# Inverse's second product in its own PSUM bank, row exponentials moved, the gate stage in a written order, first rows convolved in two parts, five value buffers

## The chip, the cores and the metric

The kernel runs on one core of a Trainium2 chip. Times are device microseconds of one execution. Five engines work side by side: TensorE (PE, with its weight loads PEld), VectorE (DVE), ScalarE (ACT), GpSimd (POOL) and SyncE (SP), which here only issues transfers. Each works through its own instructions in order.

## The reference, cut to what matters

One step of a two-layer encoder over 2048 prompt tokens and 32 sample tokens, 2080 in all, with 1024 channels. The first layer is a gated delta rule with 8 heads of 128 channels; the second, windowed attention, is not touched by the change.

```python
proj = x @ w_in                                              # q, k, v: 3 x 1024; gate z: 1024; a, b: 2 x 8
qkv, new_buf = causal_conv(proj[..., :CONV_DIM], conv_buf, conv_w)   # 4 taps, then silu
g = -exp(a_log) * softplus(a_in + dt_bias)                   # one decay for each head and token
# the delta rule, in chunks: gcum = cumsum(g)
decay = exp(where(incl, gcum_i - gcum_j, -inf))
lower = where(strict, kbeta k^T * decay, 0); tmat = lower + I
u = triangular_solve(tmat, v * beta);  w = triangular_solve(tmat, kbeta * exp(gcum))
v_new = u - w S;  o = (q exp(gcum)) S + (q k^T * decay) v_new;  S = S exp(glast) + kdec^T v_new
o = o * rsqrt(mean(o * o)) * norm_w * silu(z)
x = layer_norm(alpha * x + o @ w_out)
```

## The kernel before, in words

All of it is one program on one core; `program` (L1644) calls the stages one after the other.

**Projections and convolutions** (`qkv`). The 2080 tokens are five blocks of 416. The 3072 channels of q, k and v are 24 rows of 128. A row of one block is 24 matmuls (8 steps over the input channels, each as three products of float parts, L77, L78, L79, to which both operands were split before) into one PSUM bank. Six banks take turns (`ps`). ACT copies each block (L297) into the row's buffer R; there are two such buffers, so row 2 takes that of row 0. Rows 0 and 1 are multiplied together, block by block, while the activations are still being read and split (L69) and two gate columns are formed (L239, L240). Then each row is convolved: the first tap by ACT (L264), the other three by DVE over all 2083 columns (L266), then tanh on ACT (L269) and a product on DVE (L270), and the row is stored. For q and k, ACT squares it, DVE transposes the squares into R (L279) and sums them (L280); that sum is the last to read R. Weights of later stages are split beside it (L95 on ACT, L96 on DVE, stored by SP at L97).

**Gate stage** (`z`, L299, and `split_gate`, L316). For 8 heads and the blocks 0, 1 and 2 the same 24 matmuls form z; block k of this stage means the k-th of these 24, counted from 0. ACT takes tanh (L309) into zth, DVE multiplies (L310) and combines (L311) into z, and SP stores it (L312). zth and z have two buffers each. The weights of the next head are fetched by SP into w_raw (L46, one buffer), cast by ACT into w_hi (L53), the rest subtracted by POOL into w_lo (L54); w_hi and w_lo have two buffers. SP also stores both for later (L323). Beside it PE gets the first steps of the delta rule for the first two chunks (`Ahead.inverses`, L955): loads of gb and k, decays E (L530 on DVE, L536 on ACT), the product g (L550) and the triangular inverse by 31 elimination steps on DVE (L573, L576). The order of PE is written out, as so many quarter blocks between two steps of `inverses`; that of DVE and ACT is left to the scheduler.

**Delta rule** (`Delta.run`, L795). 17 chunks, one of the 32 sample tokens and 16 of 128. The order on PE, DVE and ACT is written out as a list of generators; `go(v, r, ...)` takes one step of each. At any time three chunks are under way: one gets its outputs, the next one its inverse of blocks, the one after its decays, its product g and its eliminations. Of those POOL does the first 25 columns and DVE the last six (L573, L576, on both engines). `invert` (L646) joins 32 x 32 inverses to 128 x 128 ones through PSUM: y1p (L660), read by ACT (L662), up (L671, L672), read by ACT (L673) and DVE (L675, L676), y2p (L684), read by ACT (L685, L686), u2p and u2q (L693, L694), read by ACT (L695, L696). y1p, up, y2p and u2p use pool pb, which has one bank; u2q uses pool pc, which has two and also serves ks (L703 to L706) and vp (L716, L718). `powers` (L619) takes the exponential of the two gb tiles on ACT (L624); `fade` multiplies k and q by them on DVE (L632). `turn_k` transposes k and scales it on ACT (L589), `turn_v` transposes v on PE (L600). v and z tiles are loaded by SP (L520) into one ring of three buffers, `vz`. Matmuls of the gate's remaining blocks and, later, of the first output projection fill PE between the steps; for the latter SP loads x into r (L1008).

After it come the rest of the output projection, the second layer's projections and the attention, unchanged.

Of the kernel before, what the change touches and what calls it, by code (L numbers as in the profile page):

```python
# [22 lines left out]
NT = NP + NS  # L23
# [134 lines left out]
def drain(gen):  # L158
    for _ in gen:
        pass  # L160


class P1:
# [49 lines left out]
    def qkv(self):  # L213
# [12 lines left out]
        for b in range(NB):  # L226
# [14 lines left out]
            for i in range(2):  # L241
                self.block(Rs[i], self.w0[i], b)
        gates(nc, I, T, G, abT, gtmp, one, self.pt)
        parts = one.tile([128, 8, NT // 32], F32, tag="parts", name="parts")
        early, due = presplit(nc, one, I, T), 0.0
        for i in range(24):
            kind, h = i // 8, i % 8
            if i < 2:
                R = Rs[i]
            else:  # L250
                w = split_weights(nc, self.wp, I["w_in"][i], nc.gpsimd)
                R = self.row(i)
                for b in range(NB):
                    self.block(R, w, b)
            due += 224 / 20 if i >= 4 else 0
# [6 lines left out]
            W = NT + 3  # L262
            y = big.tile([128, NT + 3], F32, tag="y", name="y")
            nc.scalar.activation(y[:], R[:, 0:W], AF.Copy, scale=self.convw[:, i, 0:1])  # L264
            for j in range(1, 4):
                nc.vector.scalar_tensor_tensor(out=y[:], in0=R[:, j:j + W], scalar=self.convw[:, i, j:j + 1], in1=y[:],  # L266
                                               op0=ALU.mult, op1=ALU.add)
# [16 lines left out]
        nc.sync.dma_start(self.O["conv"][:, :, :], self.convo[:])  # L284

# [179 lines left out]
class Delta:  # L465
# [42 lines left out]
    def load(self, ch, name, halves=(0, 1)):  # L508
        nc, T, n = self.nc, self.T, ch.n
        ts = slice(ch.t0, ch.t0 + n)  # L510
        pool, tag, bufs = (self.sml, "vz", 3) if name in "vz" else (self.four, name, 5 if name == "q" else 4)
# [134 lines left out]
    def invert(self, ch):  # L646
# [7 lines left out]
        def new(pool):  # L654
            return pool.tile([128, 8, 64], F32, tag="tr", name="bps")
# [24 lines left out]
        y2p = new(self.pb)  # L680
# [114 lines left out]
    def run(self, chunks, S, first, second, side, done):  # L795
# [46 lines left out]
        for i in range(len(chunks) + 1):  # L842
# [29 lines left out]
            go(a, t, a, t, seen, sq)  # L872
            fill(2 * more)
# [25 lines left out]
            p = gen(self.powers, n2)  # L899
            go(v, r, r, r, g, r, r, v, r, k, r, d)  # L900
            side()
            go(v, w, r, d, p)
# [40 lines left out]
class Ahead(Delta):  # L943
# [11 lines left out]
    def inverses(self, chunks):  # L955
        for ch in chunks:
            tmp = Chunk(ch.t0, ch.n)
            for name in ("gb", "k"):
                self.load(tmp, name)
            yield  # L960
            drain(self.decays(tmp))
            yield
            low = self.lower(tmp)
            next(low)
            yield
            drain(low)
            drain(self.chain(tmp, self.nc.vector, 0, 31))
# [676 lines left out]
def program(tc, I, O, T, G):  # L1644
# [7 lines left out]
    zs = p1.z((0, 1, 2), zp, ("zth", "z"), p1.ps, p1.split_gate(nc.gpsimd))  # L1652
    ahead = Ahead(tc, mid, left, I, O, T, G).inverses(chunks[:2])
    with tc.manual_schedule(engines={mybir.EngineType.PE}):
        for n in (18, 18, 6, 6, 12, 12):
            next(ahead)
            drain(itertools.islice(zs, n))
        drain(ahead)
        drain(zs)
# [52 lines left out]
    ET = mybir.EngineType  # L1712
# [191 lines left out]
```

## Time and profile before

| | |
|---|---|
| three runs | 2224.55, 2231.66, 2234.78 us; median 2231.66 |
| profiled execution | 2230.72 us |
| its span in the profile | 2228.9 us |
| mean granted TensorE clock | 0.983 |
| busy: PE, PEld | 2111.1, 1919.0 us |
| busy: DVE, ACT, POOL | 1479.8, 909.8, 718.5 us |
| L266, 72 convolution steps on DVE | 173.3 us |
| L573, L576 on POOL, 375 steps each | 127.8, 143.0 us |

Busy time counts an engine as working while one of its instructions runs; matmuls overlap, so a busy PE may still be slow. A row of a timeline gives start, duration, engine, line, operation, outputs <- inputs, size, and in brackets how long the engine was idle before it and whose result ended the idle time. Groups ("x4") are runs of like instructions. A "q" behind an engine's name is its instruction queue, where transfers are issued. The granted clock is a share of full speed.

### The profile page before, as it was taken

The numbers are of one execution on the slowest core, as the hardware profiler recorded it, in microseconds if no ns is written. First come the engines' busy times: TensorE is split into PE (matmuls) and PEld (weight loads), VectorE is DVE, ScalarE is ACT, GpSimd is POOL, SyncE is SP. The second block draws the span as 40 slices with busy tenths as digits, with TensorE's granted clock in tenths as the row PEclk, the third lists the DMA queues.
The fourth block names the chain that finished last, engine by engine and source line by source line (L and its number), as shares of the span: only waits on it lengthen the run. The fifth ranks groups of instructions, "written<-read, shape, count | busy, mean of one in ns | idle before, by whom it ended". The sixth has DMA issues, their size and how long they took to land.

```text
span 2228.9 us, 37186 instructions
## 1 busy us (share of the span) xinstructions
PE 2111.1 (95%) x13370; PEld 1919.0 (86%) x13370; DVE 1479.8 (66%) x2765; ACT 909.8 (41%) x2403; POOL 718.5 (32%) x1176
## 2 busy tenths in 40 slices
PE   8999999999989999888789999899999998999997
PEld 6899999999989888887777887899999976888775
DVE  4798877876656688778865665554844566556662
ACT  5555545444422566666651211311311035444441
POOL 1223211161110377777751210000000035566663
PEclk9999999999999999999999999999999999999999
DMA  7656656567865534434746765888788895333321
GB/s 285 211 192 190 206 172 194 183 194 232 260 215 175 170 130 148 150 128 157 238 130 233 247 209 157 290 285 283 254 290 287 270 298 157 103 88 95 91 76 43
DMA packets 348377, 430.00 MB, mean 193 GB/s; under 512 B 78352, under 2 KB 276080, under 8 KB 348176
## 3 DMA queue, kind: packets, MB, share of 16 engines
q1 hardware_dynamic: 311280, 310.22, 43.9%
q10 hardware_dynamic: 36912, 117.40, 15.8%
q8 instruction: 106, 1.74, 0.3%
q14 instruction: 79, 0.65, 0.1%
HBM read 269.45 MB, written 158.44 MB: 192 GB/s over the span
## 4 chain that ended last, share of the span: by engine, by line
PE 71%; DVE 13%; DMA 6%; ACT 5%; issue 3%; SPq 2%; POOL 1%; ACTq 0%; DVEq 0%; POOLq 0%
PE ps L77 8%; PE ps L79 8%; PE ps L78 8%; PE ps L1257 5%; PE ps L1258 5%; PE ps L1259 5%; PE ot L1611 3%; PE po L1498 3%; PE po L1499 3%; PE po L1500 3%; PE S L1590 2%; PE po L1030 2%; PE po L1032 2%; PE po L1031 2%; PE tr L1605 2%
## 5 line engine op out<-in xcount | busy, mean ns | idle before, releaser
L77 PE MATMUL ps<-act_hi,w_hi 128*128 128x416 f32 x1280 | 459.4, 359 | 10.0 <-DVE z L310 5.8
L79 PE MATMUL ps<-act_hi,w_lo 128*128 128x416 f32 x1280 | 450.4, 353 | 2.1 <-POOL w_lo L54 1.2
L78 PE MATMUL ps<-act_lo,w_hi 128*128 128x416 f32 x1280 | 451.7, 353 | 0.0
L77 PEld LDWEIGHTS ps<-act_hi,w_hi 128*128 128x128 f32 x1280 | 242.3, 189 | 14.5 <-DVE z L310 6.1
L79 PEld LDWEIGHTS ps<-act_hi,w_lo 128*128 128x128 f32 x1280 | 242.3, 189 | 6.3 <-POOL w_lo L54 1.7
L78 PEld LDWEIGHTS ps<-act_lo,w_hi 128*128 128x128 f32 x1280 | 243.0, 190 | 2.7
L1257 PE MATMUL ps<-xs_h,w 128*128 128x416 f32 x560 | 199.6, 356 | 11.4 <-DVE ra L1314 7.4
L1258 PE MATMUL ps<-xs_l,w 128*128 128x416 f32 x560 | 199.9, 357 | 3.2 <-DVE xs_l L1160 3.2
L1259 PE MATMUL ps<-xs_h,w 128*128 128x416 f32 x560 | 198.5, 355 | 0.0
L54 POOL TENSOR_TENSOR w_lo<-w_raw,w_hi 128x1024 fp32r<-128x1024 f32 x32 | 83.9, 2622 | 343.0 <-ACT w_hi L53 342.9
L266 DVE SCALAR_TENSOR_TENSOR y<-R,convw,y 128x2083 f32<-128x2083 f32 x72 | 173.3, 2408 | 21.3 <-ACT y L264 21.1
L573 POOL TENSOR_TENSOR tm<-L,Tt 128x60 f32<-128x60 f32 (+19 forms) x375 | 127.8, 341 | 118.3 <-PE sp L748 45.6
L576 POOL TENSOR_TENSOR Tt<-Tt,tm 128x60 f32<-128x60 f32 (+19 forms) x375 | 143.0, 381 | 28.3
L1598 POOL TENSOR_TENSOR P<-P,sm 128x384 f32<-128x384 f32 (+2 forms) x128 | 100.9, 810 | 119.8 <-DVE sm L1477 56.6
L1452 POOL MEMSET vd<- 64x768 f32 (+2 forms) x10 | 7.8, 779 | 397.0 <-DVE ra L1314 396.7
L1473 ACT ACTIVATE P<-S,nm 128x192 f32<-128x192 f32 (+2 forms) x260 | 104.6, 419 | 60.7 <-DVE nm L1466 48.2
L1257 PEld LDWEIGHTS ps<-xs_h,w 128*128 128x128 f32 x560 | 106.5, 190 | 14.4 <-DVE ra L1314 8.1
L1314 DVE SCALAR_TENSOR_TENSOR ra<-ps,u 128x416 f32<-128x416 f32 x60 | 35.4, 590 | 122.9 <-PE ps L1259 122.0
L1030 PE MATMUL po<-wo,g_hi 128*128 128x512 f32 (+1 forms) x272 | 110.2, 405 | 4.1 <-DVE r L1035 3.1
L1258 PEld LDWEIGHTS ps<-xs_l,w 128*128 128x128 f32 x560 | 106.3, 190 | 5.6 <-DVE xs_l L1160 4.2
L1259 PEld LDWEIGHTS ps<-xs_h,w 128*128 128x128 f32 x560 | 106.9, 191 | 1.3
L1032 PE MATMUL po<-wo,g_lo 128*128 128x512 f32 (+1 forms) x272 | 106.7, 392 | 0.0
(298 smaller groups left out, 4778.3 us busy)
## 6 DMA issues: line engine op xcount, KB each, us to landing
w<-s_w ACTq DMA_DIRECT2D x180, 512.0 KB
s_w<-pre_hl SPq DMA_DIRECT2D x160, 256.0 KB
w_raw<-in_w_in SPq DMA_DIRECT2D x32, 512.0 KB
s_wo<-pre_hl SPq DMA_DIRECT2D x64, 256.0 KB
gb<-s_gcum SPq DMA_DIRECT2D x34, 256.0 KB
k<-s_k SPq DMA_DIRECT2D x34, 256.0 KB
s_z<-z SPq DMA_DIRECT2D x40, 208.0 KB
s_q<-y SPq DMA_DIRECT2D x8, 1024.0 KB
```

The lines of the kernel that those rows point to most:

```text
L77: nc.tensor.matmul(ps, hi[:, k, :], xh[:, k, :], start=(k == 0), stop=False)
L78: nc.tensor.matmul(ps, hi[:, k, :], xl[:, k, :], start=False, stop=False)
L79: nc.tensor.matmul(ps, lo[:, k, :], xh[:, k, :], start=False, stop=(k == KC - 1))
L266: nc.vector.scalar_tensor_tensor(out=y[:], in0=R[:, j:j + W], scalar=self.convw[:, i, j:j + 1], in1=y[:], op0=ALU.mult, op1=ALU.add)
L573: P.tensor_tensor(out=tm[:n, i0 - k:, :w], in0=L[:n, i0:, j:j + 1].to_broadcast(sh), in1=Tt[:n, j:j + 1, :w].to_broadcast(sh), op=ALU.mult)
L576: P.tensor_tensor(out=Tt[:n, i0:, :w], in0=Tt[:n, i0:, :w], in1=tm[:n, i0 - k:, :w], op=ALU.subtract)
L1030: nc.tensor.matmul(ps[:n], ghi[:, k, :n], w[0][k][:, cs], start=(k == 0), stop=False)
L1032: nc.tensor.matmul(ps[:n], glo[:, k, :n], w[0][k][:, cs], start=False, stop=(k == KC - 1))
L1257: nc.tensor.matmul(ps, w[:, 0, k], xh[:], start=first and k == 0, stop=False, skip_group_check=True)
L1258: nc.tensor.matmul(ps, w[:, 0, k], xl[:], start=False, stop=False, skip_group_check=True)
L1259: nc.tensor.matmul(ps, w[:, 1, k], xh[:], start=False, stop=last and k == 3, skip_group_check=True)
L1473: nc.scalar.activation(P[u], src, AF.Exp, bias=nm[:, u:u + 1], scale=1.0, accum_out=sm[:, u:u + 1])
```

## The change

Five edits, made together.

1. In `invert`, y2p is allocated in pool pc (tag sc) instead of pb.
2. `powers` of the chunk after next is no longer one of the generators of the second `go` list behind `spread`, but is run right after the output steps, before the errors and `spread`.
3. In the gate stage the order of DVE and ACT is written out too. `inverses` yields how many quarter blocks follow: 36 first, then 2, 2 and 16 times 2 between four elimination steps each, for the second chunk 2, 2 and 16 times 1. The second chunk's loads are issued after the first one's product. The weights of the gate's heads 0 and 1 are fetched and split within the last row of `qkv`, by the same generator, which is then handed on.
4. Rows 0 and 1 are convolved in two parts by a new method `conv`: columns 0 to 1248 after block 2, the rest at the old place.
5. The ring `vz` has five buffers instead of three.

```diff
@@ -240,6 +240,10 @@
                 nc.vector.tensor_tensor(out=abT[:n, t, :], in0=abT[:n, t, :], in1=tp[:n, :16], op=ALU.add)
             for i in range(2):
                 self.block(Rs[i], self.w0[i], b)
+            if b == 2:
+                ys = [big.tile([128, NT + 3], F32, tag="y", name="y") for i in range(2)]
+                for i in range(2):
+                    self.conv(ys[i], Rs[i], i, 0, 3 * TB)
         gates(nc, I, T, G, abT, gtmp, one, self.pt)
         parts = one.tile([128, 8, NT // 32], F32, tag="parts", name="parts")
         early, due = presplit(nc, one, I, T), 0.0
@@ -250,8 +254,14 @@
             else:
                 w = split_weights(nc, self.wp, I["w_in"][i], nc.gpsimd)
                 R = self.row(i)
+                if i == 23:
+                    gate = self.split_gate(nc.gpsimd)
+                    first = next(gate)
                 for b in range(NB):
                     self.block(R, w, b)
+                if i == 23:
+                    next(gate)
+                    self.gate = itertools.chain([first, None], gate)
             due += 224 / 20 if i >= 4 else 0
             while due >= 1 or i == 23:
                 due -= 1
@@ -259,12 +269,8 @@
                     break
             nc.gpsimd.tensor_copy(self.convo[:, i, 0:3], R[:, NP:NP + 3])
             nc.gpsimd.tensor_copy(self.convo[:, i, 3:6], R[:, NT + 3:NT + 6])
-            W = NT + 3
-            y = big.tile([128, NT + 3], F32, tag="y", name="y")
-            nc.scalar.activation(y[:], R[:, 0:W], AF.Copy, scale=self.convw[:, i, 0:1])
-            for j in range(1, 4):
-                nc.vector.scalar_tensor_tensor(out=y[:], in0=R[:, j:j + W], scalar=self.convw[:, i, j:j + 1], in1=y[:],
-                                               op0=ALU.mult, op1=ALU.add)
+            y = ys[i] if i < 2 else big.tile([128, NT + 3], F32, tag="y", name="y")
+            self.conv(y, R, i, 3 * TB if i < 2 else 0, NT + 3)
             th = one.tile([128, NT + 3], F32, tag="th", name="th")
             nc.scalar.activation(th[:], y[:], AF.Tanh, scale=0.5)
             nc.vector.scalar_tensor_tensor(out=y[:], in0=th[:], scalar=1.0, in1=y[:], op0=ALU.add, op1=ALU.mult)
@@ -282,6 +288,12 @@
             if h == 7:
                 norms(nc, G, parts, self.sel, kind, one, self.pt)
         nc.sync.dma_start(self.O["conv"][:, :, :], self.convo[:])
+
+    def conv(self, y, R, i, a, z):
+        self.nc.scalar.activation(y[:, a:z], R[:, a:z], AF.Copy, scale=self.convw[:, i, 0:1])
+        for j in range(1, 4):
+            self.nc.vector.scalar_tensor_tensor(out=y[:, a:z], in0=R[:, a + j:z + j], scalar=self.convw[:, i, j:j + 1],
+                                                in1=y[:, a:z], op0=ALU.mult, op1=ALU.add)
 
     def row(self, i):
         R = self.big.tile([128, NT + 6], F32, tag="R", name="R")
@@ -508,7 +520,7 @@
     def load(self, ch, name, halves=(0, 1)):
         nc, T, n = self.nc, self.T, ch.n
         ts = slice(ch.t0, ch.t0 + n)
-        pool, tag, bufs = (self.sml, "vz", 3) if name in "vz" else (self.four, name, 5 if name == "q" else 4)
+        pool, tag, bufs = (self.sml, "vz", 5) if name in "vz" else (self.four, name, 5 if name == "q" else 4)
         tiles = ch.__dict__.setdefault(name, [])
         for q in halves:
             hs = slice(q * 4, q * 4 + 4)
@@ -677,7 +689,7 @@
         V.tensor_copy(self.ub[0:32, :, 0:32], ucp[64:96, 4:8])
         V.tensor_copy(self.ub[32:64, :, 32:64], ucp[96:128, 4:8])
         yield
-        y2p = new(self.pb)
+        y2p = self.pc.tile([128, 8, 64], F32, tag="sc", name="bps")
         low, high = slice(0, 64), slice(64, 128)
         for p in range(4):
             for q, dst in ((p, high), (p + 4, low)):
@@ -870,6 +882,8 @@
                 self.load(n3, "q", (0,))
             side()
             go(a, t, a, t, seen, sq)
+            if n2:
+                drain(self.powers(n2))
             fill(2 * more)
             if i + 2 == len(chunks):
                 for q in range(2):
@@ -896,10 +910,9 @@
             go(g)
             fill(2 * more)
             d = gen(self.decays, n3)
-            p = gen(self.powers, n2)
             go(v, r, r, r, g, r, r, v, r, k, r, d)
             side()
-            go(v, w, r, d, p)
+            go(v, w, r, d)
             if i:
                 self.load(ch, "z")
             fill(more)
@@ -953,18 +966,27 @@
         self.constants()
 
     def inverses(self, chunks):
-        for ch in chunks:
-            tmp = Chunk(ch.t0, ch.n)
+        tmps = [Chunk(ch.t0, ch.n) for ch in chunks]
+
+        def load(tmp):
             for name in ("gb", "k"):
                 self.load(tmp, name)
-            yield
+
+        load(tmps[0])
+        yield 36
+        for i, (ch, tmp) in enumerate(zip(chunks, tmps)):
             drain(self.decays(tmp))
-            yield
+            yield 2
             low = self.lower(tmp)
             next(low)
-            yield
+            yield 2
             drain(low)
-            drain(self.chain(tmp, self.nc.vector, 0, 31))
+            if i == 0:
+                load(tmps[1])
+            chain = self.chain(tmp, self.nc.vector, 0, 31)
+            for _ in range(16):
+                drain(itertools.islice(chain, 4))
+                yield 2 - i
             ch.Tt, ch.ready = tmp.Tt, True
 
 
@@ -1649,13 +1671,12 @@
     mid.close()
     zp = new_pool(tc, left, "p1_z", 2, side="left")
     chunks = [Chunk(NP, NS)] + [Chunk(t * 128, 128) for t in range(16)]
-    zs = p1.z((0, 1, 2), zp, ("zth", "z"), p1.ps, p1.split_gate(nc.gpsimd))
+    zs = p1.z((0, 1, 2), zp, ("zth", "z"), p1.ps, p1.gate)
     ahead = Ahead(tc, mid, left, I, O, T, G).inverses(chunks[:2])
-    with tc.manual_schedule(engines={mybir.EngineType.PE}):
-        for n in (18, 18, 6, 6, 12, 12):
-            next(ahead)
+    ET = mybir.EngineType
+    with tc.manual_schedule(engines={ET.PE, ET.DVE, ET.Activation}):
+        for n in ahead:
             drain(itertools.islice(zs, n))
-        drain(ahead)
         drain(zs)
     kept = p1.kept_gate()
     next(kept)
@@ -1709,7 +1730,6 @@
     def done(ch):
         sent.add(ch.t0)
 
-    ET = mybir.EngineType
     with tc.manual_schedule(engines={ET.PE, ET.DVE, ET.Activation}):
         delta.run(chunks, S, first, second, side, done)
     right.close()
```

The order on ACT in a late chunk of the delta rule, before. `bps` are the PSUM tiles of `invert`, `ta`, `yb` and `u` what ACT makes of them, `kd` the scaled k, `gb` the tiles that `powers` exponentiates; `wo` are loads for the output projection:

```order
L662 ACTIVATE y_6423<-bps 32x256 x2
L665 COPY ta<-tcp 32x8x32 x2
L673 COPY ta<-bps 32x8x32
L589 ACTIVATE kd<-tr,t_ekd 128x128 x4
L977 DMA wo<-s_wo 128x1024
L685 COPY ta<-bps 64x256
L686 COPY yb<-bps 64x256
L689 COPY u<-tcp 32x8x32 x4
L624 ACTIVATE gb<-gb 128x512 x2
L695 ACTIVATE u<-bps 64x4x64
L696 ACTIVATE u<-bps 64x4x64
L589 ACTIVATE kd<-tr,t_ekd 128x128 x4
```

And the same place after the change (line numbers are 12 higher there):

```order
L636 ACTIVATE gb<-gb 128x512 x2
L674 ACTIVATE y_6431<-bps 32x256 x2
L677 COPY ta<-tcp 32x8x32 x2
L685 COPY ta<-bps 32x8x32
L601 ACTIVATE kd<-tr,t_ekd 128x128 x4
L999 DMA wo<-s_wo 128x1024
L697 COPY ta<-bps 64x256
L698 COPY yb<-bps 64x256
L701 COPY u<-tcp 32x8x32 x4
L707 ACTIVATE u<-bps 64x4x64
L708 ACTIVATE u<-bps 64x4x64
L601 ACTIVATE kd<-tr,t_ekd 128x128 x4
```

The exponentials have moved from between the copies of u and the two scalings of u to ahead of the first read of `bps`.

DVE in the first rows of `qkv`, before, from the first convolution on (R is a row, y its convolution, gtmp the gate columns, pre_hl split weights):

```order
L359 TENSOR_TENSOR gtmp<-gtmp,g_dt 128x136
L266 SCALAR_TENSOR_TENSOR y<-R,convw,y 128x2083
L360 SCALAR_TENSOR_TENSOR gtmp<-gtmp 128x136
L266 SCALAR_TENSOR_TENSOR y<-R,convw,y 128x2083 x2
L362 TENSOR_SCALAR gtmp<-gtmp 128x136
L96 TENSOR_TENSOR pre_hl<-pre_raw,pre_hl 128x256 x2
L266 SCALAR_TENSOR_TENSOR y<-R,convw,y 128x2083
L96 TENSOR_TENSOR pre_hl<-pre_raw,pre_hl 128x256 x2
L266 SCALAR_TENSOR_TENSOR y<-R,convw,y 128x2083
L363 RECIPROCAL gtmp<-gtmp 128x136
L270 SCALAR_TENSOR_TENSOR y<-th,y 128x2083
L266 SCALAR_TENSOR_TENSOR y<-R,convw,y 128x2083
```

DVE after the change, from the last split of the activations on:

```order
L69 TENSOR_TENSOR act_lo_185<-act_raw,act_hi_184 128x1664
L295 SCALAR_TENSOR_TENSOR y<-R,convw,y 128x1248
L239 COPY gtmp<-tp 128x16
L295 SCALAR_TENSOR_TENSOR y<-R,convw,y 128x1248
L240 TENSOR_TENSOR gtmp<-gtmp,tp 128x16
L96 TENSOR_TENSOR pre_hl<-pre_raw,pre_hl 128x256 x4
L295 SCALAR_TENSOR_TENSOR y<-R,convw,y 128x1248
L239 COPY gtmp<-tp 128x16
L240 TENSOR_TENSOR gtmp<-gtmp,tp 128x16
L239 COPY gtmp<-tp 128x16
L240 TENSOR_TENSOR gtmp<-gtmp,tp 128x16
L295 SCALAR_TENSOR_TENSOR y<-R,convw,y 128x1248 x2
```

The first 1248 columns of both rows now come right behind that split, among the gate columns of the later blocks; the other 835 follow behind the last block, at the old place.

ACT at the start of the gate stage, before, from the last row's tanh on (zth is the gate's tanh, w_hi a head's weights, E a decay, Tt the start of an inverse):

```order
L269 ACTIVATE th<-y 128x2083
L53 CAST w_hi<-w_raw 128x1024
L95 CAST pre_hl<-pre_raw 128x256 x4
L274 DMA s_v<-y 128x32
L309 ACTIVATE zth<-ps 128x416 x2
L53 CAST w_hi<-w_raw 128x1024
L309 ACTIVATE zth<-ps 128x416 x2
L558 COPY Tt<-tinit 32x256
L558 COPY Tt<-tinit 128x256
L536 ACTIVATE E<-E,t_ngc 32x32 x8
L309 ACTIVATE zth<-ps 128x416 x2
L53 CAST w_hi<-w_raw 128x1024
```

And after (line numbers 12 higher, the row's tanh 6):

```order
L275 ACTIVATE th<-y 128x2083
L95 CAST pre_hl<-pre_raw 128x256 x4
L280 DMA s_v<-y 128x32
L321 ACTIVATE zth<-ps 128x416 x4
L53 CAST w_hi<-w_raw 128x1024
L321 ACTIVATE zth<-ps 128x416 x3
L53 CAST w_hi<-w_raw 128x1024
L321 ACTIVATE zth<-ps 128x416
L548 ACTIVATE E<-E,t_ngc 32x32 x8
L321 ACTIVATE zth<-ps 128x416
L567 COPY nb<-npr 32x256
L570 COPY Tt<-tinit 32x256
```

The cast of head 1's weights has left this place; each later cast stands behind the tanh of the first block of the head before, and the decays E behind the tanh of block 7 (counted from 0).

## The prediction

> **What bounds the kernel now.** I read the page first, for the engine that sets the time; then the chain of waits, then PE's waits by releaser, then the stages in windows, and last the timelines of PE, ACT, DVE, POOL and SP round each wait that the change touches.
>
> ```profile
> span 2228.9 us, 37186 instructions
> PE 2111.1 (95%) x13370; PEld 1919.0 (86%) x13370; DVE 1479.8 (66%) x2765; ACT 909.8 (41%) x2403; POOL 718.5 (32%) x1176
> ...
> PE 71%; DVE 13%; DMA 6%; ACT 5%; issue 3%; SPq 2%; POOL 1%; ACTq 0%; DVEq 0%; POOLq 0%
> ```
>
> PE is busy 95% of the span, and its instructions hardly change: no matmul is added or removed. So the change can only win PE's idle time and the time PE runs slowly. These are PE's waits that it touches (sum us, times, longest):
>
> ```profile
> PE bps L684 <- DVE ub L676: 18.3, 16, 1.8
> ...
> PE g L550 <- ACT kd L589: 5.9, 9, 1.4
> PE ps L77 <- DVE z L310: 5.8, 1, 5.8
> ...
> PE ps L77 <- ACT R L297: 3.8, 1, 3.8
> ...
> PE vtr L600 <- DMA v<-s_v: 2.7, 1, 2.7
> ...
> PE vp L716 <- ACT u L695: 1.0, 1, 1.0
> ```
>
> Together 37.5 us. The windows (PE, PEld, DVE, ACT, POOL busy; granted clock; DMA share; GB/s) show the stages: convolutions, gate stage, an early and a late stretch of the delta rule.
>
> ```profile
> 50.00:100.00 50.00, 50.00 (x264) 46.93 (x264) 31.84 (x52) 20.77 (x38) 8.07 (x7) 1.00 0.64 204
> ...
> 600.00:650.00 50.00, 44.20 (x231) 42.62 (x230) 24.86 (x32) 16.18 (x37) 8.40 (x3) 0.93 0.76 238
> 800.00:850.00 50.00, 45.48 (x489) 42.55 (x489) 40.48 (x93) 29.87 (x99) 36.30 (x96) 0.87 0.43 142
> 1100.00:1150.00 50.00, 39.10 (x489) 35.12 (x488) 40.62 (x93) 30.89 (x101) 40.66 (x105) 1.00 0.62 194
> ```
>
> In the delta rule no engine is full: PE, DVE and POOL wait for each other in turns, so a wait taken off the loop shortens it only until the next engine is in the way.
>
> **First rows convolved in two parts.** PE has filled all six PSUM banks with row 2 and the start of row 3, and waits until ACT can copy the first of them into the buffer R that row 0 had; the last reader of that buffer is a DVE reduction.
>
> ```profile
> 107.18 0.72 PE L77 MATMUL ps<-act_hi,w_hi 128*128 128x416 f32 x1 [3.83 <-ACT R L297]
> ...
> 113.18 0.35 PE L79 MATMUL ps<-act_hi,w_lo 128*128 128x416 f32 x1
> 113.37 0.35 PE L77 MATMUL ps<-act_hi,w_hi 128*128 128x416 f32 x1
> ```
> ```profile
> 106.63 0.91 ACT L297 COPY R<-ps 128x416 f32<-128x416 f32 x2
> ```
> ```profile
> 102.28 2.31 DVE L280 TENSOR_REDUCE parts<-R 128x65 f32<-128x2080 f32 x1
> ```
> ```profile
> L266 DVE SCALAR_TENSOR_TENSOR y<-R,convw,y 128x2083 f32<-128x2083 f32 x72 | 173.3, 2408 | 21.3 <-ACT y L264 21.1
> ```
>
> The stall costs more than its 3.83 us. From 107.18 to 113.18 there are 17 steps in 6.00 us; at the pitch that follows (113.18 to 113.37, 0.19) they take 3.2, so PE loses 2.8 us more at about half speed: 6.6 in all. Of the 2083 columns of each of the six steps on rows 0 and 1, 1248 (60%) move ahead: 0.6 x 2.41 = 1.44 us each, 8.7 us in all, into the stretch 50 to 100, where DVE is busy 31.84 of 50 us. Ahead of the reduction stand then 5.8 us instead of 14.4. It would end some 8 us before its 104.59, and the copy could start before PE runs dry at 103.35. If DVE's idle time were not free where the pieces land, at worst 8.7 us would come back as delay and nothing is won; six more instruction starts are a fraction of a microsecond. What is late next is row 1's buffer, with the same margin. I take +6.6, range 0 to 6.6.
>
> **Second product in its own bank; exponentials moved.** Late chunk: ACT, PE, DVE are chained through L673, L675/676, L684, L685, L689, L624, L695, L589, L550.
>
> ```profile
> 1109.28 0.76 ACT L662 ACTIVATE y<-bps 32x256 f32<-32x256 f32 x2 [3.88 <-PE bps L660]
> ...
> 1112.27 0.88 ACT L589 ACTIVATE kd<-tr,t_ekd 128x128 f32<-128x128 f32 x3
> 1113.85 0.37 ACT L685 COPY ta<-bps 64x256 f32<-64x256 f32 x1 [0.70 <-PE bps L684]
> ...
> 1116.28 0.63 ACT L624 ACTIVATE gb<-gb 128x512 f32<-128x512 f32 x1
> ...
> 1116.82 0.61 ACT L624 ACTIVATE gb<-gb 128x512 f32<-128x512 f32 x1
> ```
> ```profile
> L685 ACT COPY ta<-bps x16: 367/367/368, 768.2 to 1166.6; 64x256 f32<-64x256 f32 x16
> ...
>   PE bps L684: 12.9, 16
> ```
> ```profile
> 1103.12 0.26 POOL L573 TENSOR_TENSOR tm<-L,Tt 128x31 f32<-128x31 f32 x1 [0.83 <-DVE tm L573]
> ```
> ```profile
>   DVE tm L573: 44.5, 14
> ```
>
> PE's 18.3 us before L684 do not all come back: in its own bank the product no longer waits for DVE's copies, but ACT, which must read it, still has three transposes (L589) ahead of it. What can be won there is ACT's own idle time before L685: 0.70 in this chunk, 12.9 over the 16 (the second of the two rows on L685). The two exponentials are 1.15 us of ACT (1116.28 to 1117.43) between L689 and L695; in their new place, ahead of L662, ACT sits idle 3.88 us, so they cost nothing there, and if that cover were gone, 1.15 per chunk, 18 in all. Who waits for them, fade (L632), comes later in both. With them gone the nine waits of L550 behind L589 (5.9) and the one of L716 (1.0) should vanish. The own bank is one of the two of pc: the product takes the bank of ks, whose reader L706 is long done, and vp takes it after L686, also done, so I see no new wait; bounds 0 and one 0.70 per chunk, and I take 0.
>
> POOL sets a limit. It works through a third chunk's inverse meanwhile, and it waits for DVE at the start of each, 44.5 us over 14 chunks, but only 0.83 in the late chunk shown and again in the next. There L684 and L550 offer 0.70 + 1.40 each; only 0.83 can be taken, so 2 x 1.27 = 2.5 are lost. Value buffers: in one chunk SP holds v behind an r that has no free buffer.
>
> ```profile
> 1056.12 0.33 SPq L1008 DMA_DIRECT2D r<-in_x  x1
> ...
> 1059.49 0.32 SPq L520 DMA_DIRECT2D v<-s_v  x1
> ```
>
> With five buffers v no longer waits for its own old reader and is issued ahead of that r; the 2.7 of L600 go. Sum for the delta rule: 12.9 + 5.9 + 1.0 + 2.7 - 2.5 = 20.0. Upper end: PE's full waits, 18.3 + 5.9 + 1.0 + 2.7 = 27.9. Lower end, where POOL or DVE stop the chunks at half of the 19.8 of the first three terms and only v is full: about 10.
>
> **Gate stage in a fixed order.** PE's 5.8 us here have this cause:
>
> ```profile
> 613.14 0.58 SPq L46 DMA_DIRECT2D w_raw<-in_w_in  x1
> 613.77 0.45 SPq L323 DMA_DIRECT2D s_wz<-w_lo  x1
> ...
> 621.54 0.93 SPq L938 DMA_DIRECT2D Sp<-in_state_delta  x2
> 622.58 0.94 SPq L312 DMA_DIRECT2D s_z<-z  x2
> ...
> 641.99 0.82 SPq L312 DMA_DIRECT2D s_z<-z  x2
> ```
> ```profile
> 628.78 1.21 DVE L310 TENSOR_SCALAR z<-ps,nwh 128x416 f32<-128x416 f32 x2 [6.70 <-DMA s_z<-z]
> ...
> 643.97 0.65 DVE L310 TENSOR_SCALAR z<-ps,nwh 128x416 f32<-128x416 f32 x1 [1.50 <-DMA s_z<-z]
> ```
> ```profile
> 618.16 1.05 ACT L53 CAST w_hi<-w_raw 128x1024 fp32r<-128x1024 f32 x1 [9.73 <-DMA w_raw<-in_w_in]
> ```
> ```profile
> 619.34 2.40 POOL L54 TENSOR_TENSOR w_lo<-w_raw,w_hi 128x1024 fp32r<-128x1024 f32 x1 [10.04 <-ACT w_hi L53]
> ```
>
> The first two z tiles are stored at 622.58, behind SP's loads; they land about 6.2 us later, and DVE, ACT and PE stand still for want of a z buffer. The same stall brings the clock of this window to 0.93; as at 107.18 I count 2.8 us for it: 8.6 now. The fixed order doesn't touch SP, but head 1's weights are now loaded before: w_raw, s_wz and one Sp come out of the way of the first store, 0.58 + 0.45 + 0.47 = 1.5 us. So 5.8 becomes 4.3. In return ACT casts head 3's weights in order behind the tanh of block 6, which waits for the tile of block 2 to be stored. Counted from the landing T of the first store: 1.2 for block 2's two DVE steps, 2.0 for its store (641.99 to 643.97), 1.2 for block 4's, 1.05 for the cast, 2.40 for POOL: T + 7.9. PE wants head 3 one block (24 steps of 0.19, 4.5) after it resumes at T + 0.7: at T + 5.2, or T + 8.0 if that block runs half slow. So either 2.8 lost in the clock or 2.7 in the wait: 4.3 + 2.8 = 7.1 against 8.6, a gain of 1.5; I take +1 for a tanh more in that chain. Bounds: the store is freed wholly (+8), or both waits and two slow stretches, 4.3 + 2.8 + 4.3 + 2.8 = 14.2 (-6). Later heads have three blocks, 13.5 us, for a cast and POOL's 2.40.
>
> On these slow stretches the Trainium skill (TensorE: Matmul & The Clock Gate, HAM oscillation — how this bites in real kernels) says that an idle window of about 3.4 us puts TensorE to half clock. This trace agrees at 107.18 (3.83 us, then half speed). By it 4.3 would still cost a slow stretch and 2.7 alone would not, which is the sum as it stands.
>
> **The sum.** 6.6 + 20.0 + 1 = 27.6 us. The profiled execution took 2230.72 us (1.8 outside its span); the median of the three runs is 2231.66, so 2204. A measurement of this kernel can tell about 0.5%, 11 us, from no change.
>
> **Rivals.**
> R1, gate stage: both waits and a second slow stretch, -6 in place of +1: 2211. For: ACT's and DVE's orders are rigid now. Against: the second wait hides under the first slow stretch. Chance 0.12.
> R2, delta rule bound elsewhere: POOL's chain, or ACT's transposes, give only 10 of 20: 2214; with R1 2221. For: 0.83 of POOL's idle time. Against: the other 12 chunks hold (44.5 - 1.7) / 12 = 3.6 each. Chance 0.15.
> R3, slower: the clock of the delta rule. PE's longest wait in the window 800 to 850 is this:
>
> ```profile
> 842.04 0.69 PE L660 MATMUL bps<-tcp,npr 32*32 32x32 f32 x32 [1.02 <-DVE tcp L641]
> ```
>
> Yet the window has 0.87, and costs (1 - 0.87) x 50 = 6.5 us; the late one has 1.00. If gathering the waits at one place made the other windows alike, each costs 6.5; the stage, 768 to 1167 by the row on L685, has eight, and from six on (39 us) the gain of 27.6 and 11 more are gone: 2243. Against: fewer idle times should not cool more. Chance 0.04.
> R4, the same clock the other way: the 6.5 go and the waits come back whole, 6.6 + 27.9 + 1 + 6.5 = 42: 2190. Chance 0.09. The Trainium skill's rule above would leave no slow stretch here, since no wait is near 3.4 us; the 0.87 contradicts it.
> R5, the early convolutions don't do what they say: DVE has them when it is needed, and R stays late: 2204 + 6.6 = 2211. Chance 0.06.
>
> **Chances.** The forecast has 0.54. The range 2189 to 2222 leaves out R3, half of R4 and the tails of the rest. Faster by over 0.5% (below 2220.5) are the forecast, R1, R4, R5 but for 0.02, and two thirds of R2: 0.84. Within 0.5%: R2's rest and the double case, 0.11. Slower: R3 and what I don't see, 0.05.
>
> **What would show it.** Right: no PE wait near 107 and clock 1.00 in 100 to 150; L684's successor without a DVE wait, with ACT's idle time before L685 near 0; no L550 wait behind L589 and no DMA wait at L600; POOL's idle time before a chunk's first step shrinks; one gate-stage wait for z of about 4, and one at head 3 for the weights. Wrong: a wait of PE for a bank of pc, POOL without idle time and the chunk still 24.3 us (1103.12 to 1127.43), or clocks of 0.9 in new windows.

## The result, and the profile after

The changed kernel takes 2210.68 us (median; 2207.43 to 2212.65) against 2231.02 before (2224.55 to 2234.78): ratio 0.991, 95% interval 0.9883 to 0.9938, that is 14 to 26 us faster. The forecast was 2204, 27 us.

The page of the profiled execution (2207.43 us), its first lines and the chain by engine:

```profile
span 2205.6 us, 37189 instructions
...
PE 2101.2 (95%) x13370; PEld 1911.0 (87%) x13370; DVE 1486.4 (67%) x2771; ACT 912.1 (41%) x2405; POOL 713.6 (32%) x1176
...
PE 69%; DVE 12%; POOL 5%; DMA 5%; ACT 4%; issue 3%; SPq 1%; ACTq 0%; DVEq 0%; POOLq 0%
```

PE is busy 10 us less with the same number of instructions, so these ran faster; the other 13 of the 23.3 us between the spans are less idle time. That agrees with the mean granted clock, 0.983 before and 0.987 after: (1 - clock) x span is 38 and 29 us. On the chain POOL has gone from 1% to 5%. PE's waits, in the places of those shown before (lines after the change are 12 higher in the gate stage and the delta rule):

```profile
PE bps L705 <- ACT u L701: 8.0, 11, 0.7
...
PE ks L717 <- DVE Sp L766: 6.4, 5, 2.2
PE po L1052 <- DVE r L1057: 6.0, 1, 6.0
...
PE ps L77 <- ACT w_hi L53: 3.6, 1, 3.6
PE ps L79 <- POOL w_lo L54: 3.5, 3, 1.8
PE ps L77 <- DMA w_hi<-s_wz: 3.4, 1, 3.4
...
PE ps L77 <- DVE z L322: 2.5, 1, 2.5
PE g L562 <- ACT kd L601: 2.0, 4, 0.5
...
PE bps L696 <- ACT ta L685: 0.5, 1, 0.5
```

Two of these were shorter before:

```profile
PE ks L705 <- DVE Sp L754: 3.1, 4, 0.9
...
PE bps L693 <- ACT u L689: 1.6, 9, 0.2
```

The 18.3 us ahead of the second product are 0.5, the wait for R and that for v are gone, that for z is 2.5 instead of 5.8, that of g for the scaling copies (L562, before L550) 2.0 instead of 5.9. The one ahead of the last products of the inverse (L705, before L693) has grown to 8.0, that of ks for the state Sp to 6.4. Longer are also those for the gate's weights (3.6 for w_hi, 3.5 in three waits for w_lo), that for the first kept weights (3.4) and one in the output projection (6.0; the longest there was 2.6). The same windows as before (columns as there):

```profile
100.00:150.00 50.00, 50.00 (x271) 48.60 (x270) 41.86 (x59) 24.59 (x44) 8.05 (x10) 1.00 0.65 208
600.00:650.00 50.00, 41.37 (x213) 38.64 (x212) 24.99 (x46) 12.03 (x29) 7.11 (x3) 0.93 0.66 205
800.00:850.00 50.00, 46.89 (x551) 44.37 (x550) 44.66 (x100) 36.15 (x116) 41.66 (x106) 1.00 0.48 157
```

The convolutions now run at full clock at 100 to 150, and so does the early delta rule in this execution. The window of the gate stage is worse: 41.37 us of PE instead of 44.20.

To see where the time went I cut each profile at four events: the start of the last copy into R (L297), the first product g of the sample chunk after the gate stage, the first and the last copy of the second product (L685), and the end of the span. That last pair is, after:

```profile
L697 ACT COPY ta<-bps x16: 367/368/370, 769.4 to 1139.3; 64x256 f32<-64x256 f32 x16
...
  PE bps L696: 0.8, 1
```

| kernel | median, us | ratio to before (95%) | convolutions until | gate stage | to the delta rule | delta rule | rest |
|---|---|---|---|---|---|---|---|
| before | 2231 to 2234 | | 588.8 | 128.1 | 51.3 | 398.4 | 1062.3 |
| after | 2210.68 | 0.9910 (0.9883, 0.9938) | 582.8 | 131.6 | 55.0 | 369.9 | 1066.3 |
| after_again | 2209.15 (1 run) | | 582.7 | 131.1 | 52.1 | 375.3 | 1066.1 |
| a_only | 2218.90 | 0.9942 (0.9921, 0.9964) | 589.2 | 127.8 | 57.0 | 383.4 | 1065.3 |
| b_only | 2225.96 | 0.9973 (0.9954, 0.9992) | 588.5 | 128.1 | 57.5 | 387.7 | 1064.3 |
| ab | 2211.06 | 0.9901 (0.9876, 0.9927) | 588.6 | 127.8 | 53.2 | 376.1 | 1064.0 |
| d_only | 2227.05 | 0.9982 (0.9967, 0.9997) | 583.4 | 129.5 | 54.3 | 395.2 | 1062.7 |
| no_c | 2204.76 | 0.9881 (0.9863, 0.9900) | 583.0 | 128.5 | 50.8 | 371.2 | 1068.9 |
| no_corder | 2206.56 | 0.9893 (0.9868, 0.9919) | 583.0 | 128.5 | 50.5 | 376.7 | 1061.8 |
| no_cweights | 2220.08 | 0.9949 (0.9927, 0.9970) | 582.0 | 140.9 | 54.7 | 375.0 | 1066.4 |
| after_z4 | 2206.84 | 0.9885 (0.9855, 0.9914) | 582.9 | 125.6 | 58.4 | 375.4 | 1069.2 |
| sp_late16 | 2217.49 | 0.9942 (0.9921, 0.9963) | 582.9 | 132.8 | 62.7 | 370.3 | 1066.8 |
| z4_sp_late16 | 2214.21 | 0.9928 (0.9903, 0.9954) | 583.0 | 131.2 | 63.0 | 373.9 | 1068.8 |
| split23 | 2241.53 | 1.0039 (1.0022, 1.0056) | 583.2 | 130.8 | 57.8 | 404.3 | 1063.5 |

Each row but the medians is one profiled execution. Of the 23.3 us between the two spans, 6.0 come from the convolutions and 28.5 from the delta rule; 3.5 are lost in the gate stage, 3.7 on the way to the delta rule and 4.0 behind it.

### The profile page after: what moved, and what is told of

Read it like the earlier page. It is cut to its first block, busy times and chain, and to the rows that moved or that the text cites. A ratio compares the mean times of both kernels' runs of the same rounds, so it can differ in the third digit from the quotient of the medians.

```text
span 2205.6 us, 37189 instructions
## 1 busy us (share of the span) xinstructions
PE 2101.2 (95%) x13370; PEld 1911.0 (87%) x13370; DVE 1486.4 (67%) x2771; ACT 912.1 (41%) x2405; POOL 713.6 (32%) x1176
## 4 chain that ended last, share of the span: by engine, by line
PE 69%; DVE 12%; POOL 5%; DMA 5%; ACT 4%; issue 3%; SPq 1%; ACTq 0%; DVEq 0%; POOLq 0%
PE ps L77 7%; PE ps L79 7%; PE ps L78 7%; PE ps L1279 5%; PE ps L1280 5%; PE ps L1281 5%; PE ot L1633 3%; PE po L1520 3%; PE po L1521 3%; PE S L1612 3%; PE po L1522 3%; PE po L1052 2%; PE po L1054 2%; PE po L1053 2%; PE tr L1627 2%
## 5 line engine op out<-in xcount | busy, mean ns | idle before, releaser
L295 DVE SCALAR_TENSOR_TENSOR y<-R,convw,y 128x2083 f32<-128x2083 f32 (+2 forms) x78 | 175.3, 2247 | 24.4 <-ACT y L293 24.2
L585 POOL TENSOR_TENSOR tm<-L,Tt 128x60 f32<-128x60 f32 (+19 forms) x375 | 136.3, 363 | 87.2 <-PE sp L760 50.0
```

The source lines that it names most:

```text
L295: self.nc.vector.scalar_tensor_tensor(out=y[:, a:z], in0=R[:, a + j:z + j], scalar=self.convw[:, i, j:j + 1], in1=y[:, a:z], op0=ALU.mult, ...
L585: P.tensor_tensor(out=tm[:n, i0 - k:, :w], in0=L[:n, i0:, j:j + 1].to_broadcast(sh), in1=Tt[:n, j:j + 1, :w].to_broadcast(sh), op=ALU.mult)
```

## The experiments

Theory 1 is the prediction's: the terms add up, ACT's idle time (12.9) for the own bank, 6.9 for the exponentials. Its rivals: the loop is held elsewhere until both are done (2); the clock makes the gain (3). For the gate stage: the written order, the early weights, the buffers or SP's queue.

**a_only**: before, with

```diff
-        y2p = new(self.pb)
+        y2p = self.pc.tile([128, 8, 64], F32, tag="sc", name="bps")
```

> The kernel before with one edit: the second product in the other pool. The stretch of the delta rule is measured from the first to the last copy of that product by ACT: 398.4 us before, 369.9 after the whole change. Theory 1 (the prediction's sum: terms add up): ACT's idle time before the copy goes, 12.9 us, so 385 and 2218 in all. Theory 2 (the loop is held at another place, POOL's chain or ACT's exponentials, unless both edits are made): under 4 us, so over 394. Theory 3 (what came beyond 20 us is the granted clock of 750 to 900): some of the windows of that stretch go to 1.00 already here.

It gave 13.0 us by the medians. ACT's idle time before the copy, then what PE waits for instead:

```profile
L685 ACT COPY ta<-bps x16: 367/367/367, 774.0 to 1157.4; 64x256 f32<-64x256 f32 x16
...
  PE bps L684: 0.8, 1
```
```profile
PE bps L693 <- ACT u L689: 7.2, 10, 0.7
PE g L550 <- ACT kd L589: 7.1, 13, 1.4
```

ACT's idle time went from 12.9 to 0.8, as the sum had it, and not PE's 18.3: the waits behind the next ACT copies grew from 1.6 to 7.2 (L693) and 5.9 to 7.1 (L550). The interval of the gain is 8.0 to 17.6 us, so theory 2, which allowed under 4, falls here. Of the 15.0 us in the stretch some 6.5 go with the clock (theory 3, behind ab).

**b_only**: before, with the exponentials drained behind the output steps.

```diff
             go(a, t, a, t, seen, sq)
+            if n2:
+                drain(self.powers(n2))
...
-            go(v, w, r, d, p)
+            go(v, w, r, d)
```

> The kernel before with the row exponentials moved, nothing else. Theory 1: 5.9 + 1.0 us of waits behind ACT's scaling copies go, stretch 391.5, 2224 in all. Theory 2: the product still waits for DVE's copies 16 times, and what is won behind it shows as a longer wait there or at POOL: under 3 us. Theory 3: clocks as before, 0.87 to 0.97 in 750 to 900.

6.0 us by the medians (interval 1.8 to 10.3). The wait for DVE's copies stays, the one behind the scaling copies shrinks:

```profile
PE bps L684 <- DVE ub L676: 18.7, 16, 1.8
...
PE g L550 <- ACT kd L589: 1.9, 4, 0.5
```

**ab**: the two edits of a_only and b_only together, on the kernel before.

> Both edits in the delta rule, five value buffers and the rest left as before. Theory 1: 12.9 + 6.9 - 2.5 = 17.3 us by waits alone, stretch 381, 2214 in all. Theory 2: more than the two alone together by 5 us or more. Theory 3: 17.3 and about 8 of the clock, stretch 373, and the windows of 750 to 900 at 1.00.

20.9 us, against 13.0 + 6.0: additive within the noise. The stretch is 22.3 shorter; the sum of waits was 17.3. For theory 3, what the clock may cost is estimated as (1 - clock) x 50 summed over the eight windows from 750 to 1150: 11.5 us before, 5.0 in a_only, 8.0 in b_only, 8.5 in ab. So about 3 of ab's 22.3 us go with the clock, and two of its windows are still at 0.93: the clock does not make the gain, though it adds to it. The wait for v was still there (L600, 3.4 us; 1.7 to 3.4 in all runs with three value buffers); with five it is in none. Five buffers alone were not run.

**no_c**: the changed kernel with the gate edit undone.

```diff
-                if i == 23:
-                    gate = self.split_gate(nc.gpsimd)
-                    first = next(gate)
...
-    zs = p1.z((0, 1, 2), zp, ("zth", "z"), p1.ps, p1.gate)
+    zs = p1.z((0, 1, 2), zp, ("zth", "z"), p1.ps, p1.split_gate(nc.gpsimd))
...
-        for n in ahead:
+        for n in (18, 18, 6, 6, 12, 12):
...
```

> The changed kernel with the gate stage as before: order of DVE and ACT left to the scheduler, weights of heads 0 and 1 at the old place. If the written order costs the 3.5 us in the gate stage and the 3.7 us up to the delta rule that the trace of after shows, 2203.5 against 2210.7, and PE's waits for head 3's weights (3.55 + 1.83) and for the first kept weights (3.41) are gone. Rival: these waits follow from the 6 us by which the stage starts earlier, so that loads and stores meet otherwise; then about 2211 and the wait for z back at 5.8 or more.

2204.76, 5.9 below the changed kernel, though the two intervals of the ratio overlap. The gate stage is 128.5 instead of 131.6, and the waits for head 3's weights are gone; the wait for z is back at 7.0, longer than the 5.8 before, as the rival had it.

**d_only**: before, with rows 0 and 1 convolved in two parts.

```diff
+            if b == 2:
+                ys = [big.tile([128, NT + 3], F32, tag="y", name="y") for i in range(2)]
+                for i in range(2):
+                    self.conv(ys[i], Rs[i], i, 0, 3 * TB)
...
```

> The kernel before with the first two rows convolved in two parts. The prediction: the wait of 3.83 us at 107 and the slow 6 us behind it go, the last copy of the convolution stage moves from 588.4 to 582, all of 6.6 arrives at the end: 2225 against 2231.9. Rival: the earlier start makes the gate stage's stores wait longer (7.03 us for z in the run without the written order, 5.80 before), so that 1 to 3 us are given back: 2227 or more.

4.1 us (interval 0.7 to 7.4). The stage ends 5.4 earlier, and the next one gives 1.4 back, as the rival had it, at the wait for z, which was 5.8:

```profile
625.74 0.72 PE L77 MATMUL ps<-act_hi,w_hi 128*128 128x416 f32 x1 [7.47 <-DVE z L316]
```

**no_corder**: the changed kernel, DVE's and ACT's order in the gate stage again the scheduler's. `inverses` is taken back whole, so its counts of quarter blocks and the place of the second chunk's loads are the old ones too.

```diff
-    with tc.manual_schedule(engines={ET.PE, ET.DVE, ET.Activation}):
-        for n in ahead:
+    with tc.manual_schedule(engines={mybir.EngineType.PE}):
+        for n in (18, 18, 6, 6, 12, 12):
+            next(ahead)
...
```

> The changed kernel with DVE's and ACT's order in the gate stage left to the scheduler, the weights of heads 0 and 1 still split early. If the written order is what costs the 6 us of the gate edit: 2205, and no wait of PE for head 3's weights. If the early weights cost them (they take SP, ACT and POOL time at the end of the convolutions): 2210.

**no_cweights**: the order kept, the early weights undone.

```diff
-                if i == 23:
-                    next(gate)
-                    self.gate = itertools.chain([first, None], gate)
...
-    zs = p1.z((0, 1, 2), zp, ("zth", "z"), p1.ps, p1.gate)
+    zs = p1.z((0, 1, 2), zp, ("zth", "z"), p1.ps, p1.split_gate(nc.gpsimd))
```

> The changed kernel with the written order kept and the weights of heads 0 and 1 at their old place. If the written order costs the 6 us: 2211 or more, with the wait for head 3's weights, and now one for head 1's too (two transfers more ahead of the first store, 1.5 us). If the early weights cost them: 2205.

The gate stage takes 128.5 without the written order and 140.9 without the early weights: it is the written order, with its counts and load places, that costs, and the early weights are what it needs. Which of its parts costs the runs do not tell. Without the early weights PE waits for head 1 too:

```profile
602.88 0.72 PE L77 MATMUL ps<-act_hi,w_hi 128*128 128x416 f32 x1 [7.73 <-ACT w_hi L53]
```

**after_z4**: the changed kernel with the pool of z and zth at four buffers (the later gate blocks use it too).

```diff
-    zp = new_pool(tc, left, "p1_z", 2, side="left")
+    zp = new_pool(tc, left, "p1_z", 4, side="left")
```

> The changed kernel with four buffers for the gate's z and tanh tiles instead of two. If the chain is landing of the first z store, then block 4's tanh, block 6's tanh, the cast of head 3's weights: PE's waits for z (2.51), w_hi (3.55) and w_lo (1.83) go, and with them the slow stretch behind (clock 0.66 in 630 to 640): 8 to 11 us, 2200 to 2203. If the cast is late for another reason (the load into w_raw, or ACT's order by itself), the 5.4 us for the weights stay and at most 2.5 go: 2208.

The gate stage is 6.0 shorter, 125.6, the best of all. But only the wait for z went; head 3 still waits (PE), now because ACT waits for the fetch:

```profile
624.64 0.46 PE L77 MATMUL ps<-act_hi,w_hi 128*128 128x416 f32 x1 [2.40 <-ACT w_hi L53]
627.13 0.71 PE L79 MATMUL ps<-act_hi,w_lo 128*128 128x416 f32 x1 [1.84 <-POOL w_lo L54]
```
```profile
623.55 1.04 ACT L53 CAST w_hi<-w_raw 128x1024 fp32r<-128x1024 f32 x1 [9.71 <-DMA w_raw<-in_w_in]
```

So the chain of z buffers was one cause, and the late fetch another close behind it. In the end times the gain is not clear: the interval of 2206.84 (0.9855 to 0.9914) overlaps that of the changed kernel, and the stretch to the delta rule is 3.4 longer in this profile.

**sp_late16**: SP's order written out as well, the loads for the first decays later.

```diff
-        load(tmps[0])
-        yield 36
+        yield 16
+        load(tmps[0])
+        yield 20
...
-    with tc.manual_schedule(engines={ET.PE, ET.DVE, ET.Activation}):
+    with tc.manual_schedule(engines={ET.PE, ET.DVE, ET.Activation, ET.SP}):
```

> The changed kernel with SP's order in the gate stage written out too, and the loads for the first decays issued after block 4 instead of ahead of block 0; two z buffers as in the change. If the waits of the gate stage come from SP's queue (the first z store and head 3's fetch stand behind some ten loads): the first store lands about 6 us earlier, PE's waits for z, w_hi and w_lo of 2.51, 3.55 and 1.83 go with the slow stretch, the stage falls from 131.6 to 120 to 123 us, 2200 in all. If they come from ACT's written order or the number of buffers: over 128 us, 2208 or more. Risk: the first decays come later and stop DVE and ACT once, 1 to 3 us.

The expectation failed: 132.8. No wait for z is left, but in SP's written order the fetch of head 2's weights stands behind the third z store, whose tile DVE could not write until the first store had landed (SP, ACT, PE):

```profile
612.61 0.33 SPq L324 DMA_DIRECT2D s_z<-z  x1
612.98 0.43 SPq L46 DMA_DIRECT2D w_raw<-in_w_in  x1
```
```profile
616.91 1.04 ACT L53 CAST w_hi<-w_raw 128x1024 fp32r<-128x1024 f32 x1 [10.00 <-DMA w_raw<-in_w_in]
```
```profile
618.01 0.71 PE L77 MATMUL ps<-act_hi,w_hi 128*128 128x416 f32 x1 [9.22 <-ACT w_hi L53]
```

**z4_sp_late16**: that, with the four z buffers of after_z4 (the same line).

> As sp_late16, with four z buffers. With the queue as the cause, the buffers add little: within 2 us of sp_late16. With both as causes: another 3 us or more.

131.2; the wait for head 2 is 7.19. In both, PE also waits longer for the first kept weights (5.4 and 5.1 us), and the stretch to the delta rule is 62.7 and 63.0. What stands ahead in SP's queue decides which wait comes; neither order was a good one.

**split23**: the changed kernel, POOL two steps fewer.

```diff
-    SPLIT = 25
+    SPLIT = 23
```

> The changed kernel with POOL doing 23 instead of 25 of the 31 elimination steps, DVE eight instead of six. POOL loses about 1.4 us a chunk. If POOL holds the chunks in which it shows no idle time before its first step (the three last, 23.7 us): these get shorter, by up to 1 us, and the others, which DVE and ACT hold, longer by 0.5 to 0.9; 2211 to 2217 in all. If POOL holds no chunk: all of them longer, also the last three, 2218.

2241.53, worse than either case: the stretch is 404.3, and PE waits for DVE's last steps:

```profile
PE bps L672 <- DVE tcp L653: 23.0, 14, 2.4
```

It was 5.6 with 25. Of the late chunks the three from the twelfth interval between second products on got longer too (24.9, 24.7, 27.3 instead of 24.6, 23.6, 23.7). DVE's steps stand between POOL's end and the next inverse, so taking work from POOL lengthens that part. But the clock fell as well: (1 - clock) x 50 over the eight windows is 33.0 here, against 3.0 and 7.0 in the two profiles of the changed kernel, nearly as much as the stretch grew. The run neither separates the two costs nor tells whether POOL holds the late chunks.

**after_again**: the changed kernel a second time.

> The changed kernel once more, unaltered, for a second profile. If the 55.0 us from the first g to the first copy of the second product (51.3 before) and the wait of 3.41 for the kept weights belong to the change, they are there again within 1 us. If they vary from one execution to the next, as in the runs that leave this place alone (57.0 and 57.5 with single edits), they come out otherwise; the delta rule's stretch, 369.9, should return within the part that the clock makes, 3 us.

The stretch to the delta rule came out as 52.1, 2.9 less, with no wait of 3.4 for w_hi; the gate stage was the same within 0.5. The delta rule took 5.4 us more, where at most 3 were expected. One window of it:

```profile
800.00:850.00 50.00, 46.81 (x528) 44.18 (x527) 41.91 (x96) 33.70 (x110) 38.11 (x98) 0.93 0.45 150
```

It had 1.00 in the first profile of the same kernel. Over the eight windows, (1 - clock) x 50 is 7.0 us here and 3.0 there.

## Why the forecast was right, and where it was off

**First rows**: 6.6 foreseen, 6.0 in the profile (5.4 with this edit alone). The wait is gone, and the window 100 to 150 is at 1.00. The reduction that held the buffer ends at 93.27 instead of 104.59, and ACT's copy follows at 93.38. Before, the copy came only at 106.63: behind the reduction ACT still did two pairs of casts for which it waited on transfers, which the prediction left out. What the sum did not have is that the next stage gives a part back: it starts earlier, its loads and stores do not, and its wait for z grew from 5.8 to 7.5 with this edit alone.

**Delta rule**: 20.0 foreseen; the profiles give 28.5, or 24 if the second profile of the changed kernel and d_only, whose delta rule is the old one, are averaged in ((398.4 + 395.2) / 2 - (369.9 + 375.3) / 2 = 24.2). The choice of ACT's 12.9 rather than PE's 18.3 fits a_only, 13.0: the late chunk on ACT now runs on without a gap into the copy of the second product, and the two scalings stand right behind the copies of u.

```profile
1112.54 0.88 ACT L601 ACTIVATE kd<-tr,t_ekd 128x128 f32<-128x128 f32 x3
1113.43 0.37 ACT L697 COPY ta<-bps 64x256 f32<-64x256 f32 x1
...
1115.87 0.38 ACT L707 ACTIVATE u<-bps 64x256 f32<-64x256 f32 x1
```

The sum missed that ACT then becomes what PE waits for, 8.0 us over 11 chunks at L705, that 2.0 of the 5.9 at L550 stay, and that the wait for Sp grows by 3.3. The limit by POOL is there as foreseen. Two first steps of late chunks:

```profile
1079.26 0.27 POOL L585 TENSOR_TENSOR tm<-L,Tt 128x31 f32<-128x31 f32 x1
...
1102.92 0.28 POOL L585 TENSOR_TENSOR tm<-L,Tt 128x31 f32<-128x31 f32 x1
```

Neither has idle time in front; the chunk is 23.66 us instead of 24.31, a gain of 0.65 where 0.83 was allowed. What came on top of the 20 is the clock, rival R4 in part: (1 - clock) x 50 over the windows 750 to 1150 is 11.5 before and 12.0 in d_only, 3.0 and 7.0 in the two profiles after, some 7 less. Between those two the stretch differs by 5.4 and the clock by 4.0, with the same kernel, so it counts nearly fully there. By that estimate 24.2 less some 7, about 17.5, came from the waits, where 20.0 were foreseen. Whether the edits hold the clock up or the executions differ by chance is not settled by two profiles of each.

**Gate stage**: +1 foreseen, -3.5 measured (131.6 and 131.1 against 127.8 to 129.5 in the seven kernels with the scheduler's order). Of these seven, the three whose stage starts some 6 us earlier, as here, have 128.5 to 129.5; against these the written order costs 2 to 3 us, and the earlier start the rest. This is the step that failed, and it lay between the forecast and R1 (-6). The chain of the cast was the right one, its sizes were not (PE, SP, DVE, ACT, POOL of the changed kernel):

```profile
621.31 0.46 PE L77 MATMUL ps<-act_hi,w_hi 128*128 128x416 f32 x1 [2.51 <-DVE z L322]
629.67 0.45 PE L77 MATMUL ps<-act_hi,w_hi 128*128 128x416 f32 x1 [3.55 <-ACT w_hi L53]
632.15 0.72 PE L79 MATMUL ps<-act_hi,w_lo 128*128 128x416 f32 x1 [1.83 <-POOL w_lo L54]
```
```profile
621.90 1.59 SPq L324 DMA_DIRECT2D s_z<-z  x2
```
```profile
620.60 0.65 DVE L322 TENSOR_SCALAR z<-ps,nwh 128x416 f32<-128x416 f32 x1 [14.89 <-DMA s_z<-z]
...
626.78 0.65 DVE L322 TENSOR_SCALAR z<-ps,nwh 128x416 f32<-128x416 f32 x1 [3.63 <-DMA s_z<-z]
```
```profile
628.17 0.52 ACT L321 ACTIVATE zth<-ps 128x416 f32<-128x416 f32 x1 [4.39 <-DVE z L323]
628.59 1.04 ACT L53 CAST w_hi<-w_raw 128x1024 fp32r<-128x1024 f32 x1
```
```profile
629.75 2.35 POOL L54 TENSOR_TENSOR w_lo<-w_raw,w_hi 128x1024 fp32r<-128x1024 f32 x1 [19.97 <-ACT w_hi L53]
```

The first store lands at T = 620.60, and PE resumes at T + 0.7, as foreseen. Then block 2's store takes 4.9 us (621.90 to 626.78), where the sum had 2.0 from a later place, at which the DMA engines were busy 0.63 of the time instead of 0.83; with the tanh, POOL ends at 632.10, T + 11.5 instead of T + 7.9. The wait for z is 2.51, less than the 4.3 foreseen, and so no slow stretch hides the weights' wait; that comes after them. The windows 620 to 630 and 630 to 640:

```profile
620.00:630.00 10.00, 5.14 (x26) 4.71 (x26) 4.88 (x8) 2.87 (x5) 0.25 (x1) 1.00 0.67 260
630.00:640.00 10.00, 8.16 (x41) 6.83 (x40) 5.50 (x10) 2.24 (x10) 2.10 (x1) 0.66 0.72 244
```

After 2.51 the clock stays at 1.00, after 3.55 and 1.83 it falls. These two agree with the idle window of about 3.4 us that the Trainium skill gives (TensorE: Matmul & The Clock Gate, HAM oscillation — how this bites in real kernels). But it also falls behind shorter waits: in after_z4 to 0.54 (627 to 629) behind 2.40 and 1.84 us with 0.65 us of work between them, while in no_corder it stays at 1.00 behind a single wait of 3.09.

```profile
627.00:629.00 2.00, 1.87 (x5) 1.82 (x6) 0.92 (x3) 1.25 (x6) 0.07 (x1) 0.54 0.46 92
```
```profile
1195.15 0.47 PE L1043 MATMUL po<-wo,g_hi 128*128 128x512 f32 x1 [3.09 <-DVE r L1048]
```

So the length of one wait does not decide, and the 0.87 near 800, where the longest wait was 1.02, may be of this kind; the runs do not show it.

**Not foreseen.** On the way to the delta rule PE waits for the first kept weights, 3.4 us in this profile. It is not the change's doing as far as the runs tell: that stretch is 57.0 and 57.5 with single edits that leave it alone, 50.8 and 50.5 in two others, 55.0 and 52.1 in two profiles of the same kernel. Behind the delta rule, 4.0 us: an x tile issued at 1187.92 lands ten us later (SP, ACT, DVE of after).

```profile
1187.92 0.34 SPq L1030 DMA_DIRECT2D r<-in_x  x1
```
```profile
1187.07 3.82 ACTq L1261 DMA_DIRECT2D w<-s_w  x4
```
```profile
1197.93 0.69 DVE L1057 SCALAR_TENSOR_TENSOR r<-r,po 128x512 f32<-128x512 f32 x1 [4.64 <-DMA r<-in_x]
```

Before, the same tile took 6.65:

```profile
1216.04 0.34 SPq L1008 DMA_DIRECT2D r<-in_x  x1
```
```profile
1216.84 2.97 ACTq L1239 DMA_DIRECT2D w<-s_w  x4
```
```profile
1222.69 0.69 DVE L1035 SCALAR_TENSOR_TENSOR r<-r,po 128x512 f32<-128x512 f32 x1 [0.47 <-DMA r<-in_x]
```

In both, ACT issues four weight loads of 512 KB at nearly the same time. Before, the x tile is issued 0.80 us ahead of the first of them; after, 0.85 us behind it. All fourteen profiles sort by this: in the six with the tile ahead (before, b_only, d_only, no_corder, no_cweights, split23) it lands in 6.5 to 8.7 us, in the eight with the tile behind in 9.8 to 10.5, and PE's wait for it is 2.6 to 4.3 and 6.0 to 6.3. No run changed that order alone, so the cause is not shown by an experiment. R2 did not happen, R5 neither (6.0 of 6.6 came), R3 not: the clock went up.

The best of the kernels by its median is the change without its gate edit, 2204.76 us. So of 34.5 us won in the profile (6.0 + 28.5), 3.5 went to the gate stage (2 to 3 of it by the written order, shown), 4.0 went behind the delta rule (by the order of two queues' loads, as far as the profiles sort) and 3.7 on the way to it (chance, as far as seen); the 23.3 that are left lie within the interval of the runs. That the total came near the forecast is luck in part: against the terms of the sum, the delta rule gave 8.5 us more in the profile, about what the clock, which the sum put at nothing, may explain, and the other stages 12.8 less. The prediction's chance of faster by over 0.5% also does not add up: its own terms give 0.89, not 0.84.

## What to carry to other kernels

Where PE's wait ends at one engine, look at the next reader on the path: the idle time of that reader, not PE's wait, is what an earlier product can win at most. An order written out for engines whose inputs arrive by transfers is only as good as the order of the transfer queue, which here was still the scheduler's; price a transfer at the busiest place of its kind, not the quietest. Before the gain of one stage is summed, ask what the next stage's loads do when it starts earlier. And look at whether a load that is waited for is issued ahead of another queue's batch or behind it.

## What the runs showed of the hardware

The same kind of store, 208 KB, took 6.2 us (622.58 to 628.78 before), 4.9 (621.90 to 626.78 after) and 2.0 (641.99 to 643.97 before), while the DMA engines were busy 0.98, 0.83 and 0.63 of that time. A load of 512 KB took 6.5 to 8.7 us when it was issued just ahead of four others from another queue, and 9.8 to 10.5 just behind the first. The granted clock of one kernel differed between two profiled executions (1.00 and 0.93 in the same window), with 5.4 us in the delta rule. And two elimination steps moved from POOL to DVE cost some 29 us (ratios to before 0.9910 and 1.0039), with 33 us of (1 - clock) x 50 in the windows of the delta rule, against 3 to 7.
